# Suffix sums of the stick-breaking attention: from F32 products of the softplus to products of a rounded high part and a rest

## Chip, cores and metric

One core of a Trainium2 chip runs the whole program. The metric is the device time of one execution in microseconds (us); the median of three runs of the kernel before is 2748.29 us. Lower is better.

## What is computed

The reference is one inference step of a four-layer decoder trunk (S5, stick-breaking attention, chunked gMLP, S5, each followed by a SwiGLU block) for 512 prompt tokens and 8 sample tokens with 512 cached positions each. The change is in the attention of layer 1 alone:

```python
def sb_attend(q, k, v, q_pos, k_pos, bias):
    z = (jnp.einsum('bqhd,bkhd->bhqk', q, k).astype(jnp.float32) * (SB_HEAD_DIM ** -0.5)
         + bias.astype(jnp.float32)[None, :, None, None])
    mask = k_pos[None, :] < q_pos[:, None]
    log_not = jnp.where(mask, jax.nn.log_sigmoid(-z), 0.0)
    suffix = lax.cumsum(log_not, axis=3, reverse=True)
    log_w = jax.nn.log_sigmoid(z) + suffix - log_not
    w = jnp.where(mask, jnp.exp(log_w), 0.0).astype(v.dtype)
    return jnp.einsum('bhqk,bkhd->bqhd', w, v)
```

Since `log_sigmoid(z) - log_not` is `z`, a weight is `exp(z - S)`, where `S` is the sum of `softplus(z)` over the keys from this one on. The kernel makes `S` on TensorE: a product with a lower triangle of ones sums inside a block of 128 keys, and products with an all-ones matrix add the later blocks.

## The kernel before

Activations lie with 128 features on the partitions and the 520 tokens (512 prompt, 8 sample) as columns. Every projection is made from a high part rounded to FP32R and a rest: three matmuls for each weight tile of 128x128 and each half of the tokens (`mm`, lines 235, 236, 238). Weights come from HBM as `raw`, ScalarE rounds them to `wh` (L206) and VectorE subtracts to get `wl` (L208).

The attention stage (`attend`, L1385) runs three things at once, as generators that a planner resumes after so many microseconds of its own count of TensorE work (`self.t`, the numbers `SBH` and `SBY`); a scheduler then sets the final order on every engine.

- The query, key and value projections of the 8 head pairs (`full`).
- `sb_pipe` (L1273) for the prompt, head pair by head pair (`m` = 0 to 7), in three pieces `u` of key blocks, of 512, 384 and 384 query columns for each of the two heads. `scores(m, u)` makes the logits in PSUM, ScalarE adds the bias into `z` (L1318) and makes Abs, Exp and Ln in `e` (L1320 to L1322), VectorE completes the softplus (L1323). `weights(m, u)` multiplies `e` by the triangle `C["tri"]` (L1334) and by ones for the later key blocks (L1338), VectorE subtracts the sums from `z` (L1343), and ScalarE makes the exponential (L1344). `values(m)` multiplies `z` by the values (L1352).
- `sb_sample` (L1147) for the 8 sample tokens: 32 pages of cached keys and 32 of values are gathered by DMAs that POOL issues (L1154). POOL multiplies a page of keys by the query (L1190, two halves), VectorE reduces it (L1194); after each 8 pages come softplus and a small suffix sum (L1216, L1217), and then the products with the value pages (L1227).

For each head pair `z` of every piece has two buffers and `e` of every piece one; the key pages have four. In one head pair the suffix sums take, for each of two heads, 512 + 384 + 384 columns with the triangle and 768 + 384 + 128 with ones:

```python
later = {0: ((1, 0, 384, 128), (2, 0, 256, 256), (2, 256, 128, 384)),
         1: ((2, 0, 256, 128), (2, 256, 128, 256)), 2: ((2, 256, 128, 128),)}[u]
```

(piece, first column, columns, target column). Operands are F32, as the triangle and `self.ones` are.

## Time and profile before

| | us |
|---|---|
| median of three runs (lowest, highest) | 2748.29 (2747.35, 2749.26) |
| the profiled execution's own time | 2746.49 |
| its span in the profile | 2744.8 |
| TensorE busy over the span | 2576.6 (94%) |
| VectorE, ScalarE, POOL busy over the span | 1545.9, 1012.0, 459.1 |
| attention stage, first scores to last values | 755.8 to 1063.3 |

The span is what the profiler saw of the engines; 1.7 us of the execution lie around it. A matmul's end is modelled, so consecutive matmuls overlap in the list; how fast a run of them goes is read from start to start. An F32 matmul stands as two records, one in FP32R as one.

### The profile page before, as it was taken

The page shows a single profiled execution, that of the slowest core. Times are in us where ns is not written, and L with a number is a line of the kernel's source. Part 1 is how long each engine was busy: PE and PEld are TensorE (multiplying, and loading weights), DVE is VectorE, ACT ScalarE, POOL GpSimd, SP SyncE. Part 2 cuts the span into 40 slices and gives each one's busy share as a digit, 9 for nine tenths or more (in the row PEclk, how much of TensorE's full clock was granted, in tenths as well). Part 3 has the DMA queues.
Part 4 walks back from the last instruction along what each step waited for, and adds up shares of the span by engine and source line. Part 5 has one row for each costly group of instructions (what it writes and reads, how often), then busy time and mean ns, then how long its engine had stood idle before and what let it go on. Part 6 is the DMA issues. An engine that isn't in the chain of part 4 may idle for free.

```text
span 2744.8 us, 49994 instructions
## 1 busy us (share of the span) xinstructions
PE 2576.6 (94%) x20922; PEld 2457.4 (90%) x20922; DVE 1545.9 (56%) x2703; ACT 1012.0 (37%) x1713; POOL 459.1 (17%) x487
## 2 busy tenths in 40 slices
PE   7769999999998899999999989999999889999998
PEld 6659999999986667999999889999999779999998
DVE  8883553434647854734345778565646755634344
ACT  5443333222344454432223564433324333432222
POOL 5661210000128820300000203000001111200000
PEclk8879999999999999999999999999999999999999
DMA  4533223333147643233333333344333544233331
GB/s 118 146 87 90 80 80 106 93 93 91 41 134 243 222 147 93 66 103 94 93 92 63 90 101 90 114 135 141 116 110 123 167 129 124 66 104 92 90 90 46
DMA packets 483073, 295.48 MB, mean 108 GB/s; under 512 B 52296, under 2 KB 458080, under 8 KB 482848
## 3 DMA queue, kind: packets, MB, share of 16 engines
q1 hardware_dynamic: 473632, 258.73, 33.1%
q0 software_dynamic: 9216, 33.56, 3.5%
q8 instruction: 165, 2.70, 0.4%
q14 instruction: 60, 0.49, 0.1%
HBM read 262.51 MB, written 29.72 MB: 106 GB/s over the span
## 4 chain that ended last, share of the span: by engine, by line
PE 73%; DVE 11%; DMA 5%; ACT 4%; POOL 3%; issue 2%; SPq 0%; ACTq 0%; DVEq 0%; POOLq 0%
PE pp L235 22%; PE pp L236 22%; PE pp L238 22%; POOL kp L1190 1%; DVE wl L208 1%; DMA raw<-in_w_ffn_in_dram 1%; DVE pn L423 1%; DVE x L425 1%; ACT wh L206 1%; PE pp L1338 1%; PE pp L1334 1%; DVE hm L925 1%; POOL x L425 1%; DMA rot<-rotd 1%; DMA wn<-wnd 1%
## 5 line engine op out<-in xcount | busy, mean ns | idle before, releaser
L235 PE MATMUL pp<-xh,wh 128*128 128x264 f32 (+1 forms) x4480 | 1209.0, 288 | 26.5 <-DVE u L1008 6.0
L236 PE MATMUL pp<-xl,wh 128*128 128x264 f32 (+1 forms) x4480 | 1210.6, 286 | 6.6 <-DVE xl L408 6.4
L238 PE MATMUL pp<-xh,wl 128*128 128x264 f32 (+1 forms) x4480 | 992.7, 286 | 6.2 <-POOL wl L208 5.6
L235 PEld LDWEIGHTS pp<-xh,wh 128*128 128x128 f32 x4480 | 853.5, 191 | 40.9 <-issue 14.1
L236 PEld LDWEIGHTS pp<-xl,wh 128*128 128x128 f32 x4480 | 854.5, 191 | 11.9 <-DVE xl L408 9.7
L206 ACT ACTIVATE wh<-raw 128x1024 fp32r<-128x1024 f32 (+2 forms) x384 | 391.3, 1023 | 1080.4 <-PE pp L236 724.7
L238 PEld LDWEIGHTS pp<-xh,wl 128*128 128x128 f32 x4480 | 738.7, 191 | 9.7 <-POOL wl L208 5.8
L208 DVE TENSOR_TENSOR wl<-raw,wh 128x1024 fp32r<-128x1024 f32 (+2 forms) x364 | 442.6, 1218 | 292.8 <-ACT wh L206 290.2
L236 PE MATMUL pp<-hl,wh 128*128 128x256 f32 (+1 forms) x1408 | 377.2, 283 | 0.0
L235 PE MATMUL pp<-hh,wh 128*128 128x256 f32 (+1 forms) x1408 | 376.7, 284 | 0.0
L238 PE MATMUL pp<-hh,wl 128*128 128x256 f32 (+1 forms) x1408 | 312.9, 283 | 0.0
L235 PEld LDWEIGHTS pp<-hh,wh 128*128 128x128 f32 x1408 | 265.1, 188 | 1.2 <-issue 1.2
L236 PEld LDWEIGHTS pp<-hl,wh 128*128 128x128 f32 x1408 | 265.3, 188 | 0.0
L238 PEld LDWEIGHTS pp<-hh,wl 128*128 128x128 f32 x1408 | 230.7, 188 | 0.0
L1622 DVE TENSOR_TENSOR tg<-pp,rs 128x520 f32<-128x520 f32 (+2 forms) x100 | 62.5, 632 | 215.4 <-PE pp L238 215.3
L1633 DVE TENSOR_TENSOR tg<-pp,tg 128x520 f32<-128x520 f32 (+2 forms) x96 | 62.4, 652 | 209.2 <-PE pp L238 208.6
L1645 DVE TENSOR_TENSOR op<-pp,op 128x520 f32<-128x520 f32 (+2 forms) x96 | 54.0, 563 | 168.1 <-PE pp L238 167.9
L340 POOL TENSOR_TENSOR acc<-acc,s 128x256 f32<-128x256 f32 (+1 forms) x96 | 83.7, 872 | 99.2 <-ACT s L336 95.3
L208 POOL TENSOR_TENSOR wl<-raw,wh 128x1024 fp32r<-128x1024 f32 x20 | 48.2, 2414 | 303.6 <-ACT wh L206 274.4
L407 ACT ACTIVATE xh<-x,gt 128x264 fp32r<-128x264 f32 (+1 forms) x128 | 63.0, 505 | 60.8 <-DVE x L425 42.5
L408 DVE SCALAR_TENSOR_TENSOR xl<-x,gt,xh 128x264 fp32r<-128x264 f32 (+1 forms) x128 | 76.7, 615 | 1.4 <-ACT xh L407 1.2
L336 ACT ACTIVATE sq<-op 128x256 f32<-128x256 f32 (+2 forms) x72 | 32.6, 453 | 101.4 <-DVE op L1645 68.4
(342 smaller groups left out, 2701.0 us busy)
## 6 DMA issues: line engine op xcount, KB each, us to landing
raw<-in_w_ffn_in_dram SPq DMA_DIRECT2D x176, 512.0 KB
raw<-in_w_ffn_out_dram SPq DMA_DIRECT2D x48, 512.0 KB
raw<-in_w_ffn_out_dram SPq DMA_DIRECT2D x48, 384.0 KB
raw<-in_w_ssm_glu_dram SPq DMA_DIRECT2D x32, 512.0 KB
raw<-in_w_sb_qkv_dram SPq DMA_DIRECT2D x24, 512.0 KB
raw<-in_w_ssm_in_dram SPq DMA_DIRECT2D x16, 512.0 KB
raw<-in_w_cm_in_dram SPq DMA_DIRECT2D x16, 512.0 KB
cad<-caw SPq DMA_DIRECT2D x16, 288.0 KB
```

The source lines that it names most:

```text
L206: nc.scalar.activation(wh[:, :nk], raw[:, :nk], AF.Copy)
L208: on.tensor_tensor(wl[:, :nk], raw[:, :nk], wh[:, :nk], op=ALU.subtract)
L235: nc.tensor.matmul(ps(*h), lhsT=wh[:, k, :], rhs=xh[:, h[0]:h[1]], start=first, stop=False)
L236: nc.tensor.matmul(ps(*h), lhsT=wh[:, k, :], rhs=xl[:, h[0]:h[1]], start=False, stop=False)
L238: nc.tensor.matmul(ps(*h), lhsT=wl[:, k, :], rhs=xh[:, h[0]:h[1]], start=False, stop=last)
L340: i = (nc.gpsimd if pool else nc.vector).tensor_tensor(acc[0][:, c0:c1], acc[0][:, c0:c1], sq[:, :n], op=ALU.add)
L407: nc.scalar.activation(xs[k][0][:, c0:c1], self.x[k][:, c0:c1], AF.Copy, scale=g)
L408: return nc.vector.scalar_tensor_tensor(xs[k][1][:, c0:c1], self.x[k][:, c0:c1], g, xs[k][0][:, c0:c1], op0=ALU.mult, op1=ALU.subtract)
L425: add.tensor_tensor(self.x[k][:, c0:c1], self.x[k][:, c0:c1], t[:, :n], op=ALU.add)
L1622: v.tensor_tensor(g, ps(c0, c1), rs[:, c0:c1], op=ALU.mult)
L1633: v.tensor_tensor(t, ps(c0, c1), t, op=ALU.mult)
L1645: v.tensor_tensor(o, ps(c0, c1), o, op=ALU.add)
```

## The change

The softplus `e` is split as the activations of the projections are: ScalarE copies it into an FP32R tile `h` and VectorE writes the difference into an FP32R tile `l`. Each F32 product with the triangle or with ones becomes two FP32R products, one of `h` and one of `l`, which add up in PSUM. Triangle and ones are held in FP32R; the sample's small sums read the same matrices as F32. To make room, `e` is one tile for the three pieces, `z` of pieces 0 and 1 has one buffer and not two, the key pages have three buffers and not four, and some small tiles share buffers of the pool `nrm`. `values(m)` is issued ahead of `scores(m + 1, 1)`, where it stood behind it.

```diff
     def consts(self):
...
-        self.ones = c.tile([128, 128], F32, name="ones")
-        nc.vector.memset(self.ones, 1.0)
+        one = self.nrm.tile([128, N], F32, tag="sq", name="one")[:, :128]
+        nc.vector.memset(one, 1.0)
+        self.onesr = c.tile([128, 128], F32R, name="ones")
+        nc.vector.tensor_copy(self.onesr, one)
+        self.ones = self.onesr.bitcast(F32)
...
     def sb_consts(self, p):
...
-        C["tri"] = p.tile([128, 128], F32, name="atri")
-        nc.gpsimd.affine_select(out=C["tri"], in_=self.ones, pattern=[[-1, 128]], compare_op=ALU.is_ge, fill=0.0,
+        tri = self.nrm.tile([128, N], F32, tag="sq", name="atri")[:, :128]
+        nc.gpsimd.affine_select(out=tri, in_=self.ones, pattern=[[-1, 128]], compare_op=ALU.is_ge, fill=0.0,
                                 base=0, channel_multiplier=1)
+        C["tri"] = p.tile([128, 128], F32R, name="atrir")
+        nc.vector.tensor_copy(C["tri"], tri)
...
-        pg = p.tile([128, 32], I32, name="apg")
+        pg, io = (self.nrm.tile([128, 264], F32, tag="pn", name="apg")[:, :32].bitcast(I32) for _ in range(2))
         nc.sync.dma_start(pg, self.i["page_table"].rearrange("b c -> (b c)").partition_broadcast(128))
-        io = p.tile([128, 32], I32, name="aio")
...
     def sb_sample(self, qf, C, p, res, first):
...
-            t = p.tile([128, D], F32, tag=nm, name=nm, bufs=4 if nm == "kp" else 3)
+            t = p.tile([128, D], F32, tag=nm, name=nm, bufs=3)
...
         def scores(m, u):
...
-            z = T[m]["z", u] = p.tile([128, 2 * n], F32, tag=f"z{u}", name=f"z{u}")
-            e = T[m]["e", u] = p.tile([128, 2 * n], F32, tag=f"e{u}", name=f"e{u}", bufs=1)
+            z = T[m]["z", u] = p.tile([128, 2 * n], F32, tag=f"z{u}", name=f"z{u}", bufs=1 + (u > 1))
+            e = p.tile([128, 1024], F32, tag="e", name="e", bufs=1)[:, :2 * n]
...
             v.scalar_tensor_tensor(e, z, 0.0, e, op0=ALU.max, op1=ALU.add)
+            hi = T[m]["h", u] = p.tile([128, 2 * n], F32R, tag=f"h{u}", name=f"h{u}", bufs=1)
+            nc.scalar.activation(hi, e, AF.Copy)
+            lo = T[m]["l", u] = p.tile([128, 2 * n], F32R, tag=f"l{u}", name=f"l{u}", bufs=1)
+            v.tensor_tensor(lo, e, hi, op=ALU.subtract)
 
         def weights(m, u):
...
-                nc.tensor.matmul(o[:, :n], lhsT=C["tri"], rhs=T[m]["e", u][:, n * h:n * h + n], start=True, stop=False)
+                for q in "hl":
+                    nc.tensor.matmul(o[:, :n], lhsT=C["tri"], rhs=T[m][q, u][:, n * h:n * h + n], start=q == "h", stop=False)
...
-                    nc.tensor.matmul(o[:, to:to + x], lhsT=self.ones, rhs=T[m]["e", w][:, W[w] * h + c:W[w] * h + c + x],
-                                     start=False, stop=(w, c) == later[-1][:2])
+                    for q in "hl":
+                        nc.tensor.matmul(o[:, to:to + x], lhsT=self.onesr, rhs=T[m][q, w][:, W[w] * h + c:W[w] * h + c + x],
+                                         start=False, stop=q == "l" and (w, c) == later[-1][:2])
...
             if old:
                 weights(m, 0)
                 yield SBH[1]
+            if old:
+                values(m)
             if new:
                 scores(m + 1, 1)
                 yield SBH[2]
-            if old:
-                values(m)
-            if new:
                 weights(m + 1, 2)
```

The scheduler makes a new order of the attention stage from this; the rest of the program keeps its order. Three places matter. In the rows that follow a name before the arrow is what is written, `L` numbers of the changed kernel are 3 to 10 higher than those before.

On POOL, where the sample part begins (the gathers of key pages and their products), before:

```order
L1154 DMA kp<-in_cache_k_dram,arow 128x1024 x4
L1291 COPY smpk<-kf_7606 128x8
L1190 TENSOR_TENSOR kp<-kp,qb 128x512 x8
L1291 COPY smpv<-v 128x8
L1154 DMA kp<-in_cache_k_dram,arow 128x1024 x4
L1190 TENSOR_TENSOR kp<-kp,qh 128x512 x2
L1291 COPY smpk<-kf_7605 128x8
L1190 TENSOR_TENSOR kp<-kp,qh 128x512 x6
L1154 DMA kp<-in_cache_k_dram,arow 128x1024 x4
```

and now:

```order
L1158 DMA kp<-in_cache_k_dram,arow 128x1024 x3
L1295 COPY smpk<-kf_7608 128x8
L1194 TENSOR_TENSOR kp<-kp,qb 128x512 x6
L1295 COPY smpv<-v 128x8
L1158 DMA kp<-in_cache_k_dram,arow 128x1024 x3
L1194 TENSOR_TENSOR kp<-kp,qb 128x512 x2
L1194 TENSOR_TENSOR kp<-kp,qh 128x512 x2
L1295 COPY smpk<-kf_7607 128x8
L1194 TENSOR_TENSOR kp<-kp,qh 128x512 x2
L1158 DMA kp<-in_cache_k_dram,arow 128x1024 x3
```

Pages are gathered and multiplied in bursts of three instead of four.

On VectorE, around the first softplus of the sample part (`em`), between two weight splits (`wl`), before:

```order
L208 TENSOR_TENSOR wl<-raw,wh 128x1024
L1203 TENSOR_SCALAR em<-zs 128x128
L1206 TENSOR_TENSOR em<-em 128x128
L1208 MEMSET em 128x2x16
L1425 TENSOR_TENSOR v<-pp,rs 128x520
L1210 TENSOR_TENSOR em<-em 128x2x16 x3
L1194 TENSOR_REDUCE zs<-kp 128x16
L1343 TENSOR_TENSOR z_8673<-z_8673,pp 128x768
L1323 SCALAR_TENSOR_TENSOR e_8779<-z_8778,e_8779 128x1024
```

and now:

```order
L1207 TENSOR_SCALAR em<-zs 128x128
L1198 TENSOR_REDUCE zs<-kp 128x16
L1327 SCALAR_TENSOR_TENSOR e<-z_8824,e 128x1024
L1210 TENSOR_TENSOR em<-em 128x128
L1212 MEMSET em 128x2x16
L1214 TENSOR_TENSOR em<-em 128x2x16 x3
L1331 TENSOR_TENSOR l_8834<-e,h_8832 128x1024
L1426 TENSOR_TENSOR kf_7608<-pp,rs 128x520
L1223 TENSOR_TENSOR zs<-zs,pss 128x128
L211 TENSOR_TENSOR wl<-raw,wh 128x1024
L1198 TENSOR_REDUCE zs<-kp 128x16
```

The new subtract (L1331) stands a few instructions behind the softplus that it splits, with reductions of key pages (L1198) and a weight split (L211) in the same queue behind it.

On TensorE, the sums of piece 0 of head pair 6, before:

```order
L1334 MATMUL pp<-e_10268,atri 128x512 x2
L1338 MATMUL pp<-e_10172,ones 128x384
L1338 MATMUL pp<-e_10100,ones 128x256
L1338 MATMUL pp<-e_10100,ones 128x128
L1338 MATMUL pp<-e_10172,ones 128x384
L1338 MATMUL pp<-e_10100,ones 128x256
L1338 MATMUL pp<-e_10100,ones 128x128
```

and now:

```order
L1343 MATMUL pp<-h_10477,atrir 128x512
L1313 MATMUL pp<-q,kf_7608 128x384 x2
L1316 LDWEIGHTS amnb
L1316 MATMUL pp<-aidb,amnb 128x128
L1316 LDWEIGHTS amnb
L1316 MATMUL pp<-aidb,amnb 128x128
L1343 MATMUL pp<-l_10479,atrir 128x512
L1343 MATMUL pp<-h_10477,atrir 128x512
L1343 MATMUL pp<-l_10479,atrir 128x512
L1348 MATMUL pp<-h_10384,ones 128x384
L1348 MATMUL pp<-l_10386,ones 128x384
L1348 MATMUL pp<-h_10283,ones 128x256
```

There are twice as many products, and the first one of `h` stands ahead of other work (here the next scores) that fills the time until `l` is there.

## Rows read from the trace of the kernel before

**Rows 1.** The page: shares of the span in the chain that ended last.

```profile
PE 73%; DVE 11%; DMA 5%; ACT 4%; POOL 3%; issue 2%; SPq 0%; ACTq 0%; DVEq 0%; POOLq 0%
```

**Rows 2.** PE, PEld, DVE, ACT, POOL busy (count), 808 to 965 us; clock, DMA.

```profile
808.00:965.00 157.00, 138.51 (x912) 98.99 (x912) 121.13 (x119) 72.67 (x110) 136.51 (x119) 0.95 0.68 223
```

**Rows 3.** TensorE over time, piece 0 of pair 6: start, length, line, count.

```profile
1029.56 1.94 PE L1334 MATMUL pp<-e,atri 128*128 128x512 f32 x4
1031.34 2.76 PE L1338 MATMUL pp<-e,ones 128*128 128x384 f32 x12
1034.03 0.64 PE L1227 MATMUL psv<-vp,zs 128*32 128x256 f32 x8
```

**Rows 4.** TensorE over time, a projection behind the stage: 34 such starts.

```profile
1098.09 0.28 PE L236 MATMUL pp<-xl,wh 128*128 128x264 f32 x1
...
1102.09 0.28 PE L236 MATMUL pp<-xl,wh 128*128 128x264 f32 x1
```

**Rows 5.** Instructions on e by stretch: PE, PEld, DVE, ACT busy (count); clock.

```profile
808.00:965.00 157.00, 39.43 (x144) 25.91 (x144) 19.30 (x12) 32.94 (x36) 0.95 0.68 223
965.00:1066.00 101.00, 32.90 (x124) 21.05 (x124) 9.41 (x9) 24.65 (x27) 1.00 0.35 106
```

**Rows 6.** Groups of ScalarE in the stage: count | busy, mean ns of one.

```profile
L1320 ACT ACTIVATE e<-z 128x768 f32<-128x768 f32 x16 | 13.5, 843 | 34.4 <-PE pp L1338 34.2
...
L1320 ACT ACTIVATE e<-z 128x1024 f32<-128x1024 f32 x8 | 8.6, 1070 | 0.0
```

**Rows 7.** VectorE over time before POOL works: the softplus, two sizes.

```profile
765.42 0.96 DVE L1323 SCALAR_TENSOR_TENSOR e<-z,e 128x768 f32<-128x768 f32 x1 [1.53 <-ACT e L1322]
...
775.02 1.22 DVE L1323 SCALAR_TENSOR_TENSOR e<-z,e 128x1024 f32<-128x1024 f32 x1 [1.64 <-ACT e L1322]
```

**Rows 8.** Groups of VectorE while POOL multiplies pages, 808 to 965 us.

```profile
L208 DVE TENSOR_TENSOR wl<-raw,wh 128x1024 fp32r<-128x1024 f32 x9 | 21.1, 2346 | 1.5 <-ACT wh L206 1.5
...
L1206 DVE TENSOR_TENSOR em<-em 128x128 f32<-128x128 f32 x3 | 8.8, 2920 | 0.9 <-ACT em L1205 0.8
```

**Rows 9.** VectorE and POOL in order of time around one weight split.

```profile
901.94 6.45 DVE L208 TENSOR_TENSOR wl<-raw,wh 128x1024 fp32r<-128x1024 f32 x1
...
902.19 2.51 POOL L1190 TENSOR_TENSOR kp<-kp,qh 128x512 f32<-128x512 f32 x2
...
904.79 2.50 POOL L1190 TENSOR_TENSOR kp<-kp,qh 128x512 f32<-128x512 f32 x2
```

**Rows 10.** POOL over time: last gather of a burst, and the next product.

```profile
823.26 0.94 POOL L1154 DMA_INDIRECT kp<-in_cache_k_dram,arow  x1 [0.30 <-issue]
825.44 2.67 POOL L1190 TENSOR_TENSOR kp<-kp,qh 128x512 f32<-128x512 f32 x2 [1.23 <-DMA kp<-in_cache_k_dram,arow]
```

**Rows 11.** POOL in order of time: its last product of a key page.

```profile
962.47 2.54 POOL L1190 TENSOR_TENSOR kp<-kp,qh 128x512 f32<-128x512 f32 x2
```

**Rows 12.** TensorE over time: the last small suffix sum of the sample.

```profile
997.48 0.39 PE L1216 MATMUL pss<-em,atri 128*128 128x128 f32 x2
```

**Rows 13.** TensorE in order of time: values of head pair 4 and of 5.

```profile
978.59 2.37 PE L1352 MATMUL po<-z,tokv 128*64 128x512 f32 x16
...
1011.19 2.37 PE L1352 MATMUL po<-z,tokv 128*64 128x512 f32 x16
```

**Rows 14.** All engines in order of time: the end of head pair 7.

```profile
1049.77 1.23 DVE L1323 SCALAR_TENSOR_TENSOR e<-z,e 128x1024 f32<-128x1024 f32 x1 [0.92 <-ACT e L1322]
...
1051.05 1.98 PE L1334 MATMUL pp<-e,atri 128*128 128x512 f32 x4 [3.19 <-DVE e L1323]
...
1060.89 2.37 PE L1352 MATMUL po<-z,tokv 128*64 128x512 f32 x16
```

**Rows 15.** VectorE in order of time just ahead of the stage.

```profile
740.87 0.19 DVE L1132 SCALAR_TENSOR_TENSOR arow<-apg,aio 128x32 int32<-128x32 int32 x1
...
742.72 0.16 DVE L359 TENSOR_SCALAR v<-psn 128x2 f32<-128x2 f32 x1 [1.00 <-PE psn L357]
```

**Rows 16.** TensorE's first instruction of the program.

```profile
7.02 0.45 PE L113 MATMUL psg<-ident,g 128*128 128x128 f32 x1 [7.02 <-DMA pin<-in_ssm_lambda_im_dram]
```

More of the change, by code (lines that the diff above doesn't have):

```diff
@@ L1215, in weights @@
             ps = self.bk.tile([128, 512], F32, tag="b", name="pss")[:, :128]
-            nc.tensor.matmul(ps, lhsT=C["tri"], rhs=em[:, 128:256], start=True, stop=False)
+            nc.tensor.matmul(ps, lhsT=C["tri"].bitcast(F32), rhs=em[:, 128:256], start=True, stop=False)
             nc.tensor.matmul(ps, lhsT=self.ones, rhs=em[:, :128], start=False, stop=True)
@@ L1237, in times_v @@
                 v.tensor_tensor(av, av, C["own"].unsqueeze(2).to_broadcast([128, 4, 64]), op=ALU.mult)
-                sums[b] = p.tile([128, 64], F32, tag="sv", name="sv")
+                sums[b] = p.tile([128, 64], F32, tag="sv", name="sv", bufs=1)
                 v.tensor_reduce(sums[b], av.rearrange("p i d -> p d i"), axis=AX.X, op=ALU.add)
@@ L1454, in attend @@
             self.t += 0.5
-            so = p1.tile([128, D], F32, tag="kp", name="so", bufs=4)
+            so = p1.tile([128, D], F32, tag="kp", name="so", bufs=3)
             nc.scalar.activation(so[:NS], pt[:NS], AF.Copy)
```

## Prediction

> **What bounds the kernel now.** I read the chain of waits first: TensorE holds 73% of what ended last [rows 1], so a saving on TensorE counts wherever nothing else ends later. The change touches the attention stage alone, so I then read the busy time by stretch and the order of time there. The stage has three stretches. From 755 to 808 us TensorE works through query projections. From 808 to 965 us POOL multiplies the key pages of the samples: POOL is busy 136.5 of 157 us, VectorE 121.1, TensorE 138.5, and the clock granted to TensorE is 0.95, where 1.00 is the higher of its two levels, 2.4 GHz [rows 2]. No engine alone sets this stretch: the reader is to see three queues that hand work to each other. From 965 to 1066 us POOL is done [rows 11], the clock is 1.00 [rows 5], and head pairs follow each other at 32.6 us (the values of pairs 4 and 5, [rows 13]) and then at 24.9 us (from pair 5 at 1011.19 to pair 7 at 1060.89 us, two steps, [rows 13, 14]). There TensorE sets the pace.
>
> **The products.** For piece 0 the columns per head are 512 + 768, for both heads 2560; its products run from 1029.56 to 1034.03 us, 4.47 us, which is 1.75 ns a column [rows 3]. One head pair has 2 x (1280 + 1280) = 5120 columns, eight have 40,960: 71.5 us of F32 products. An FP32R product of 264 columns starts every 0.121 us (33 steps from 1098.09 to 1102.09 us), 0.46 ns a column [rows 4]. Two of them for one F32 product cost 0.92 ns a column, 37.6 us: 34 us less.
>
> The unknown is the short product. Three pieces in each head have 128 columns: 48 F32 products, 96 FP32R ones. No FP32R product in the trace is below 256 columns. By columns one costs 0.059 us. At worst it costs what the F32 product of as many columns does, 0.22 us, 15.5 us more in all. I take 0.121 us, the nearest row of its kind [rows 4], since each product loads its weights anew, loads and products being as many [rows 2]: 96 x 0.062 = 6 us more. TensorE thus has **28 us** less to do (18.5 to 34). The Trainium skill, "TensorE: Matmul & The Clock Gate", section on LDWEIGHTS, says that a weight load takes as long as its columns at 1.2 GHz, whatever the rows: an estimate of 0.107 us for 128 columns, which would bind a product of 128 columns; the sum by it would be 29 us less. No row here shows it for so short a product.
>
> The 144 F32 products on `e` are 288 records, of which 144 lie in the middle stretch and 124 behind it [rows 5], so 20 ahead of it: 14.0, 12.1 and 1.9 us of the 28.
>
> **The split.** It adds 24 copies on ScalarE, 16 of 0.84 us and 8 of 1.07 us (the Abs of the same size, [rows 6]), 22 us, and 24 subtracts on VectorE, 16 of 0.96 us and 8 of 1.22 us (the softplus of the same size, [rows 7]), 25 us. Both lie between the softplus and its products, so each piece is ready some 2 us later plus what its queues hold. The new order lets `h` of the triangle go first and puts other work ahead of `l`.
>
> From 755 to 808 us the queues of both engines are short; I keep the whole 1.9 us.
>
> From 965 us on, other products cover the split, but for the last pair, whose piece 0 is a chain with nothing beside it: softplus at 1049.77, sums at 1051.05, values at 1060.89 us [rows 14]. Its sums get 2.3 us shorter (half of 4.5) and the split adds 1.07 + 1.22. So 12.1 - 2.3 = 9.8 us remain. The single buffers of `z` close a loop: from the sums of piece 0 over subtract, exponential, values, then bias, Abs to Ln, softplus, copy and subtract of piece 1, the same of piece 0, to the next sums. By the rows of these sizes (1.22, 1.06, 2.4; 1.1, 2.5, 0.96, 0.84, 0.96; 3.2, 1.22, 1.07, 1.22; 2.3) that is 20 us. Pairs now take 25 to 33 us and would take 21 to 29: the loop just fits, with nothing over for a queue. The bounds for this stretch are therefore 0 and 12.1.
>
> From 808 to 965 us lie 12 of the 24 subtracts (as many as softplus there, [rows 5]). Undisturbed they are 4 x 1.22 + 8 x 0.96 = 12.6 us. But VectorE instructions with two SBUF inputs stretch here: the weight split takes 2.35 us on the mean, a 128-column addition 2.92 us [rows 8], and one split that begins at 901.94 us takes 6.45 us, until POOL's products that begin at 902.19 have passed [rows 9]. At the split's mean of 2.35 for 1.22 us the 12 subtracts cost 24 us. VectorE has 36 us of idle time in the stretch [rows 2]. The price on the path is between 0 (idle time takes it) and 45 us (each also waits as the 128-column addition does: 128 of the 768 columns that take 0.96 us would be 0.16, so 2.7 us of its 2.92 are waiting). With 11 us of copies on ScalarE in the same chains, I take 14 us, a little over half of the 24: nothing of the 14.0 us saved there is left.
>
> **The rest.** Key pages come in bursts of three: behind a burst of four POOL waits 1.23 us for the first page [rows 10], behind three about 2.5, since one gather less (0.94 us and 0.30 ahead of it) covers it. Some four such bursts give 5 us and as many as 10 all through, on POOL. The cover: the last small sum of the sample runs at 997.48 us [rows 12], 32 us behind POOL's last product at 965.0 [rows 11]. If TensorE came to that sum 20 us sooner, it would still fit, so I take 0 (0 to 5). The page table now waits for a buffer of `nrm` and behind two weight loads on SP's queue; its user on VectorE runs at 740.87 us, and what stands behind it waits for TensorE until 742.72 us anyway [rows 15]: 0, at most 1.5 us. The extra copy of the ones, at the start, hides behind the DMA that TensorE waits for until 7.02 us [rows 16]. Moving `values` ahead of `scores` lets `z` be freed early; it adds no work.
>
> **Sum.** -1.9 - 9.8 + (14 - 14.0) = -11.7 us from the profiled execution's own 2746.5: 2734.8. The median shown is 1.8 us above that execution, so the forecast is **2737 us**.
>
> **Rivals.**
> - *All of it comes through* (-28 us, 2720). For it: VectorE's idle time in the middle stretch, and the scheduler's products of `h` that wait for nothing. Against it: [rows 8], and the loop of 20 us. It needs the split to cost nothing in any queue.
> - *Nothing is left* (2743 to 2753). The loop holds the pairs at their old pace from 965 us on, or the short products cost 0.22 us each and take another 9.5 us. For it: the pairs' 24.9 us against 20 with no queue; no row for the short products.
> - *Slower by VectorE's queue.* Place: 808 to 965 us. A subtract has two SBUF inputs; when POOL multiplies, it holds VectorE's queue until POOL pauses, and with it the reduction behind it, for which POOL's next gather waits now that only three key pages have buffers. At the upper price, 45 us for 12 subtracts, the stretch gets 31 us longer and the whole 31 - 11.7 = 19 us: 2767 us. It decides against the kernel once a subtract costs the path 2.6 us or more: (14.0 + 11.7 + 5.5) / 12. For it: 2.92 and 6.45 us in [rows 8, 9]. Against it: the softplus itself stands in the same queue, and its 12 instructions took 19.3 us there, 1.6 each [rows 5]. The Trainium skill, "SBUF — State Buffer", section "Who interferes with whom", has this as a rule: a VectorE instruction with two SBUF inputs and a GpSimd instruction that reads SBUF exclude each other, and the second waits for the whole of the first. The trace agrees in [rows 9], 6.45 us where the same split takes some 1.2 us. By the rule POOL also waits when a subtract comes first, up to 1.2 us for each of the 12, which would move POOL's last product, not the sum above.
> - *The rounded products don't run in one pass.* Then TensorE gains nothing and the split is all cost. The projections' products of the same type start every 0.121 us [rows 4], so I give it 1 in 100.
>
> **How the numbers follow.** About 0.2% (5.5 us) is what a measurement of this kernel can tell from no change. The forecast's case, 6 to 22 us faster, gets 0.48 (its own range: 2726 to 2743), all of it or nearly 0.10, no change 0.22, slower 0.20 with the failed pass in it. So faster 0.58, same 0.22, slower 0.20. The range 2721 to 2756 leaves out the best 6 in 100 and the worst 13.
>
> **What would show it.** Of the products: lines with `h` and `l` at 0.92 ns a column for both together, and 128-column ones starting every 0.12 us. Of the last stretch: values of the last three pairs 21 to 29 us apart. Of the middle stretch: the stage's POOL part still ends 155 to 165 us after it began, the new subtract at a mean near 2 us there, and VectorE busy above 140 us. I am wrong if the pairs keep their old pace behind 965 us, if the middle stretch gets shorter by as much as TensorE saves, or if the subtract's mean goes beyond 2.6 us and the key pages end 20 us later or more.

## The result: 14 us slower, and the profile after

The changed kernel took 2761.71 us (median of 5 runs, 2760.23 to 2767.26), the kernel before 2749.26 us in 5 runs beside it. The ratio is 1.0051, 95% interval 1.0036 to 1.0065: slower by 14 us (10 to 18). The forecast was 2737 us with a range of 2721 to 2756, so it was wrong, on the slow side. The profiled execution took 2760.23 us of its own time, 2758.5 us of span.

TensorE's share of the chain that ended last fell from 73% [rows 1]. The page of the changed kernel:

```profile
PE 70%; DVE 11%; DMA 6%; ACT 4%; issue 3%; POOL 3%; SPq 0%; another core or an unknown queue 0%; ACTq 0%; DVEq 0%; POOLq 0%
```

The stage begins when it did, and its last values come 15.1 us later than at 1060.89 us [rows 14]; the span grew by 13.7 us, so the loss is the stage's. TensorE in order of time, the values of pairs 4, 5 and 7 (lines move by 3 to 10: values are now L1362, the products L1343 and L1348, copy L1329, subtract L1331, reduction L1198, page gather L1158):

```profile
982.85 2.38 PE L1362 MATMUL po<-z,tokv 128*64 128x512 f32 x16
...
1018.93 1.40 PE L1362 MATMUL po<-z,tokv 128*64 128x512 f32 x6
...
1076.02 1.40 PE L1362 MATMUL po<-z,tokv 128*64 128x512 f32 x6
```

The values of pair 4 lose 4.3 us against 978.59 [rows 13]; the three pairs behind them take 93.2 us in place of 82.3. So 4 us are lost up to the end of the sample part and 11 behind it, where 9.8 were to be gained. The dividing line at pair 4 is not quite like for like: counted by line in both traces, 46 more of the projections' products now stand ahead of it (from pair 0 on) and 26 fewer behind it, at 0.12 us each [rows 4] 5.6 and 3.1 us. The loss behind pair 4 is rather larger than 11 us.

**The products did what was forecast.** TensorE in order of time, piece 0 of pair 5, products with the ones:

```profile
1011.45 0.34 PE L1348 MATMUL pp<-h,ones 128*128 128x384 f32 x1
...
1012.03 0.22 PE L1348 MATMUL pp<-h,ones 128*128 128x128 f32 x1
1012.09 0.27 PE L1348 MATMUL pp<-l,ones 128*128 128x128 f32 x1
1012.20 0.39 PE L1348 MATMUL pp<-h,ones 128*128 128x384 f32 x1
...
1012.90 0.27 PE L1348 MATMUL pp<-l,ones 128*128 128x128 f32 x1
1013.01 0.33 PE L238 MATMUL pp<-xh,wh 128*128 128x256 f32 x1
```

Twelve products take 1.56 us (1011.45 to 1013.01) for what took 2.69 us in F32 [rows 3]. Two short ones take 0.17 us (1012.03 to 1012.20), 0.085 each; I had taken 0.121. The Trainium skill, "TensorE: Matmul & The Clock Gate", section "Back-to-back issue gap", gives about 81 ns a product for 128 columns in a stream of loads and products; this row agrees.

**Where the saving went.** Busy time by stretch, from the values of pair 0 to those of pair 4, and from there to those of pair 7. Columns: stretch, length, busy time with count of PE, PEld, DVE, ACT, POOL, then TensorE's granted clock (1.00 is 2.4 GHz), DMA share, GB/s. The kernel before:

```profile
825.00:978.59 153.59, 135.10 (x890) 94.33 (x889) 118.57 (x121) 72.92 (x111) 125.55 (x111) 0.94 0.67 222
978.59:1060.89 82.30, 78.03 (x537) 52.49 (x536) 37.64 (x66) 49.45 (x82) 11.51 (x14) 1.00 0.36 110
```

The changed kernel:

```profile
822.60:982.85 160.25, 133.02 (x935) 101.51 (x934) 133.58 (x131) 83.71 (x122) 133.93 (x113) 0.88 0.67 219
982.85:1076.02 93.17, 75.47 (x512) 52.53 (x511) 47.16 (x77) 58.20 (x92) 14.57 (x16) 0.84 0.30 97
```

Busy time times granted clock is an estimate of the work done. Before it is 135.10 x 0.94 + 78.03 = 205.0 us, after 133.02 x 0.88 + 75.47 x 0.84 = 180.5: **24.5 us less work**. But busy time itself fell only from 213.1 to 208.5, so by this estimate the lower clock took back 19.9 us. Idle time grew from 22.8 to 44.9 us, by 22.1. The sum, -24.5 + 19.9 + 22.1 = 17.5 us, is what these two stretches grew by. Behind the sample part the clock fell where TensorE stood idle, or just after; before, it stayed at 1.00 there throughout, also in the stretch with the most idle time:

```profile
1040.00:1050.00 10.00, 7.17 (x38) 4.51 (x37) 5.73 (x16) 8.94 (x21) 0.00 (x0) 1.00 0.20 54
```

The changed kernel, ten us each:

```profile
990.00:1000.00 10.00, 7.60 (x39) 4.29 (x39) 4.77 (x12) 5.27 (x10) 2.87 (x3) 0.56 0.73 217
...
1040.00:1050.00 10.00, 9.13 (x58) 6.25 (x57) 4.30 (x5) 4.45 (x7) 0.00 (x0) 0.88 0.00 0
1050.00:1060.00 10.00, 4.32 (x25) 3.14 (x24) 4.58 (x14) 8.83 (x21) 0.00 (x0) 0.80 0.19 52
1060.00:1070.00 10.00, 6.73 (x29) 4.73 (x28) 3.32 (x3) 4.75 (x5) 0.00 (x0) 0.51 0.05 8
```

TensorE is busy 4.32 of 10 us from 1050 us on, and in the next 10 us its mean clock is 0.51, nearly all of it at the lower level.

**What TensorE waited for behind the sample part.** The waits of TensorE from 965 to 1080 us, the longest (total, times, longest):

```profile
PE pp L1343 <- ACT h L1329: 9.4, 4, 3.3
```

So it is `h` that is late, not `l` (0.3 us in all); before, the same place waited 3.2 us, for the softplus. All engines in order of time, from one Abs of a piece 0 (pair 6) to the next (pair 7):

```profile
1029.59 1.06 ACT L1324 ACTIVATE e<-z 128x1024 f32<-128x1024 f32 x1 [0.98 <-DVE accv L1238]
...
1034.91 1.06 ACT L1329 ACTIVATE h<-e 128x1024 fp32r<-128x1024 f32 x1 [0.49 <-DVE e L1327]
...
1036.02 0.80 PE L1343 MATMUL pp<-h,atrir 128*128 128x512 f32 x1 [2.97 <-ACT h L1329]
...
1036.75 1.65 PE L1313 MATMUL pp<-q,kf 64*128 64x384 f32 x4
...
1042.82 1.22 DVE L1353 TENSOR_TENSOR z<-z,pp 128x1024 f32<-128x1024 f32 x1 [1.98 <-PE pp L1348]
...
1044.08 1.06 ACT L1354 ACTIVATE z<-z 128x1024 f32<-128x1024 f32 x1 [0.52 <-DVE z L1353]
...
1046.35 2.37 PE L1362 MATMUL po<-z,tokv 128*64 128x512 f32 x16
...
1048.20 2.19 ACT L1322 ACTIVATE z<-pp,abias 128x512 f32<-128x512 f32 x4
...
1050.74 0.87 ACT L1324 ACTIVATE e<-z 128x768 f32<-128x768 f32 x1
...
1056.60 0.96 DVE L1331 TENSOR_TENSOR l<-e,h 128x768 fp32r<-128x768 f32 x1 [0.30 <-ACT h L1329]
...
1057.59 1.06 ACT L1324 ACTIVATE e<-z 128x1024 f32<-128x1024 f32 x1 [1.02 <-DVE l L1331]
```

This loop takes 28.0 us, a pair's whole period (the pairs here are 27.4 and 29.7 us apart). Its last step shows the shared `e`: the `z` of piece 0 was there at 1050.39 us (1048.20 + 2.19), but its Abs starts at 1057.59, when the subtract of piece 1 has let `e` go.

**The middle stretch.** POOL's last product of a key page starts at 980.36 us, not at 962.47 [rows 11], 18 us later. The last small sum is two products, one with the triangle, which [rows 12] shows, and one with the ones. The second of them before, then both in the changed kernel:

```profile
1000.15 0.38 PE L1217 MATMUL pss<-em,ones 128*128 128x128 f32 x2
```

```profile
995.48 0.76 PE L1220 MATMUL pss<-em,atrir 128*128 128x128 f32 x2 [1.76 <-DVE em L1210]
...
1005.15 0.39 PE L1221 MATMUL pss<-em,ones 128*128 128x128 f32 x2
```

The first comes 2 us sooner than before, the second 5 us later; of the 32 us between POOL's end and the first, 12 are left. VectorE's groups from 808 to 965 us, the softplus before and then the changed kernel:

```profile
L1323 DVE SCALAR_TENSOR_TENSOR e<-z,e 128x1024 f32<-128x1024 f32 x4 | 10.7, 2686 | 0.0
L1323 DVE SCALAR_TENSOR_TENSOR e<-z,e 128x768 f32<-128x768 f32 x8 | 8.6, 1070 | 0.5 <-ACT e L1322 0.5
```

```profile
L211 DVE TENSOR_TENSOR wl<-raw,wh 128x1024 fp32r<-128x1024 f32 x9 | 27.8, 3094 | 1.0 <-ACT wh L209 0.8
L1327 DVE SCALAR_TENSOR_TENSOR e<-z,e 128x768 f32<-128x768 f32 x8 | 16.7, 2088 | 0.0
L1331 DVE TENSOR_TENSOR l<-e,h 128x768 fp32r<-128x768 f32 x8 | 9.0, 1125 | 0.9 <-ACT h L1329 0.9
L1327 DVE SCALAR_TENSOR_TENSOR e<-z,e 128x1024 f32<-128x1024 f32 x4 | 4.9, 1224 | 1.2 <-ACT e L1326 1.2
```

The new subtract takes 1.1 us, not the 2 I had expected. The weight split goes from 2.35 [rows 8] to 3.09 us and the softplus of 768 columns from 1.07 to 2.09, but that of 1024 columns falls from 2.69 to 1.22 us. What is stretched has changed places.

### The profile page after: what moved, and what is told of

Its sections match the earlier page's. It is cut to its first block, busy times and chain, and to the rows that moved or that the text cites. A ratio compares the mean times of both kernels' runs of the same rounds, so it can differ in the third digit from the quotient of the medians.

```text
span 2758.5 us, 50052 instructions
## 1 busy us (share of the span) xinstructions
PE 2565.2 (93%) x20922; PEld 2458.8 (89%) x20922; DVE 1572.4 (57%) x2729; ACT 1033.9 (37%) x1737; POOL 467.7 (17%) x487
## 4 chain that ended last, share of the span: by engine, by line
PE 70%; DVE 11%; DMA 6%; ACT 4%; issue 3%; POOL 3%; SPq 0%; another core or an unknown queue 0%; ACTq 0%; DVEq 0%; POOLq 0%
PE pp L238 22%; PE pp L239 21%; PE pp L241 21%; DMA raw<-in_w_ffn_in_dram 2%; DVE wl L211 1%; POOL kp L1194 1%; ACT wh L209 1%; DVE pn L426 1%; DVE x L428 1%; DMA wn<-wnd 1%; PE pp L937 1%; POOL x L428 1%; DVE hm L928 1%; PE pp L936 1%; PE pp L1343 1%
## 5 line engine op out<-in xcount | busy, mean ns | idle before, releaser
L211 DVE TENSOR_TENSOR wl<-raw,wh 128x1024 fp32r<-128x1024 f32 (+2 forms) x364 | 451.3, 1242 | 298.3 <-ACT wh L209 295.4
L211 POOL TENSOR_TENSOR wl<-raw,wh 128x1024 fp32r<-128x1024 f32 x20 | 48.2, 2418 | 316.2 <-ACT wh L209 275.2
```

The lines of the kernel that those rows point to most:

```text
L211: on.tensor_tensor(wl[:, :nk], raw[:, :nk], wh[:, :nk], op=ALU.subtract)
```

## The experiments

Ratios are against the kernel before, run beside each; 0.1% is 2.75 us. Two accounts stood against each other: **the split** costs the time (by VectorE's work, by ScalarE's copy, or by the loop over `e`), or **the room** made for it does (three key buffers, single `z`, order of values). Each edit also makes the scheduler find another order for the stage: of POOL's 154 instructions there, 152 stand in e14 in the order that they have in e1, but 117 in e13 and 116 in e5, counted from the traces. So a price below is that of an edit together with its order; no run held the order fixed.

### e1: no split

```diff
-            v.scalar_tensor_tensor(e, z, 0.0, e, op0=ALU.max, op1=ALU.add)
-            hi = T[m]["h", u] = p.tile([128, 2 * n], F32R, ...)
-            nc.scalar.activation(hi, e, AF.Copy)
-            lo = T[m]["l", u] = p.tile([128, 2 * n], F32R, ...)
-            v.tensor_tensor(lo, e, hi, op=ALU.subtract)
+            hi = T[m]["h", u] = T[m]["l", u] = p.tile([128, 2 * n], F32R, ...)
+            v.scalar_tensor_tensor(hi, z, 0.0, e, op0=ALU.max, op1=ALU.add)
```

> The changed kernel without the split: VectorE writes the softplus rounded straight into h, and every product reads h, twice, so copy and subtract are gone while the number and form of the products, all buffers and the order stay. (The rest is left out and the high part counted twice.) Accounts of the 40 us between the 28 us that the products should save and the 12 us that were lost: if the split itself costs them (ScalarE held 34 us in front of its copies, TensorE 24 us in front of h), this runs at 2722 to 2740 us; if the room made for it costs them (three key buffers, one z for the first two blocks, one e, values earlier), it stays at 2752 to 2762.

Measured: 2731.37 us, ratio 0.9925 (0.9901 to 0.9948), 21 us under before and, by the ratios, 35 under the change. Taking the split out gives this back, so the split is the cost. The same two stretches:

```profile
820.20:957.70 137.50, 121.98 (x896) 93.84 (x895) 105.13 (x116) 72.25 (x108) 118.66 (x104) 0.95 0.72 241
957.70:1040.30 82.60, 72.72 (x522) 53.39 (x521) 44.22 (x71) 52.55 (x85) 23.91 (x24) 0.90 0.41 129
```

The work is 181.3 us by the same estimate, near the change's 180.5, with 25.4 us of idle time, near the 22.8 of before. (These stretches hold 31 fewer products of the projections than the change's, some 3.7 us, so the estimate is good to some 5 us.) Even so the last three pairs take 82.6 us: with 12 us less to do TensorE idles more there, and its clock falls from 1.00 to 0.90.

### e2: the room alone

```diff
-            z = T[m]["z", u] = p.tile([128, 2 * n], F32, tag=f"z{u}", name=f"z{u}")
+            z = T[m]["z", u] = p.tile([128, 2 * n], F32, tag=f"z{u}", name=f"z{u}", bufs=1 + (u > 1))
...
-            t = p.tile([128, D], F32, tag=nm, name=nm, bufs=4 if nm == "kp" else 3)
+            t = p.tile([128, D], F32, tag=nm, name=nm, bufs=3)
```

(and `values` ahead of the scores of block 1, as in the change; `e` keeps its three tiles)

> The kernel before with the room of the change alone: three key-page buffers, one z buffer for blocks 0 and 1, values ahead of the scores of block 1; products in F32 on e as before, no split, and e not shared (it must live until the products). If the split costs the time: within 4 us of before, 2745 to 2753. If the room costs it: 2765 to 2790.

Measured: 2754.03 us, ratio 1.0009 (0.9998 to 1.0020): some 2.5 us more, not told apart from none, and 1 us above what was expected if the split costs. The room is nearly free as long as nothing else is added.

### e3: the copy on VectorE

```diff
-            nc.scalar.activation(hi, e, AF.Copy)
+            v.tensor_copy(hi, e)
```

> The changed kernel with the rounding copy on VectorE, so that softplus, copy and subtract follow each other on one engine and ScalarE is never held behind VectorE. If ScalarE's queue (34 us held in front of the copies) is what slows the pairs: 2738 to 2752. If VectorE's own work is the bound (24 more operations of about 0.8 us in an engine busy 126 of 157 us): 2765 to 2785.

Measured: 2769.02 us, ratio 1.0065 (1.0047 to 1.0082), against 1.0051 of the change. It is no faster. This does not part two cases: ScalarE's being held behind the softplus may cost nothing, or the 24 more operations on VectorE may take back what it costs.

### e4: values in their old place

```diff
-            if old:
-                values(m)
             if new:
                 scores(m + 1, 1)
                 yield SBH[2]
+            if old:
+                values(m)
```

> The changed kernel with values back behind the scores of block 1, as before the change. If the single z buffers make ScalarE wait for values (11.8 us in the trace of the change), this makes it worse: 2768 to 2785. If the early place of values holds TensorE in front of work that was ready: 2750 to 2758.

Measured: 2775.88 us, ratio 1.0090 (1.0074 to 1.0107), 11 us more than the change. With one `z`, block 1's bias must wait for the values, and the move is needed. The change's own trace shows such a wait, behind the values of pair 5:

```profile
1020.70 1.05 ACT L1322 ACTIVATE z<-pp,abias 128x384 f32<-128x384 f32 x2 [2.86 <-PE po L1362]
```

### e5: the subtract aside

The edit is shown against e1.

```diff
             v.scalar_tensor_tensor(hi, z, 0.0, e, op0=ALU.max, op1=ALU.add)
+            lo = p.tile([128, 2 * n], F32, tag=f"l{u}", name=f"l{u}", bufs=1)
+            v.tensor_tensor(lo, z, hi, op=ALU.subtract)
```

> The kernel of e1 (VectorE writes the softplus rounded into h, products read h twice) with the subtract put back on VectorE off the chain: it takes z minus h into l, which nothing reads, so VectorE works as long as in the change and no product waits for it. e1 stood 20 us under before and 31 us under the change. If VectorE's work is the cost of the split, 20 us or more of the 31 come back: 2750 to 2762. If it is the steps that stand in the chain from softplus to product: 2729 to 2738.

Measured: 2753.54 us, ratio 1.0009 (0.9998 to 1.0021): 23 us above e1, though nothing reads the result: VectorE's added work costs that, with the order that it brings. From 808 to 965 us the subtract is stretched here, as it was not in the change:

```profile
L1330 DVE TENSOR_TENSOR l<-z,h 128x768 f32<-128x768 f32 x8 | 19.4, 2421 | 0.0
```

The two stretches:

```profile
822.40:983.57 161.17, 135.57 (x926) 105.76 (x925) 130.90 (x133) 72.40 (x109) 136.74 (x113) 0.86 0.66 216
983.57:1060.94 77.37, 67.54 (x502) 49.51 (x501) 44.55 (x75) 52.40 (x85) 11.32 (x14) 0.91 0.36 117
```

The first is as long as in the change (160.25), the second 15.8 us shorter. So the subtracts alone can account for the change's middle stretch, but not for its last three pairs.

### e6: the copy in the chain

The edit is shown against e1.

```diff
-            v.scalar_tensor_tensor(hi, z, 0.0, e, op0=ALU.max, op1=ALU.add)
+            v.scalar_tensor_tensor(e, z, 0.0, e, op0=ALU.max, op1=ALU.add)
+            nc.scalar.activation(hi, e, AF.Copy)
```

> The kernel of e1 with the softplus written in F32 to e and copied to h by ScalarE, as in the change, and no subtract: the products read h twice (the rest is left out, the high part counted twice). The chain has its hop to ScalarE and e is held until the copy, VectorE has nothing more to do than in e1. If the hop and the order of ScalarE's queue are the cost: 2745 to 2762. If VectorE's work is: 2729 to 2738.

Measured: 2737.49 us, ratio 0.9955 (0.9940 to 0.9970): 8 us above e1, with intervals that overlap, and in the range of the account by VectorE. Copy and hop are the smaller part.

### e7, e8 and e9: a second `e`, a fourth key page, neither

All three hold the rest `l` in BF16, with the triangle and ones in BF16 for its products. e7 spends the room on `e`, e8 on the key pages, e9 on nothing.

```diff
-            lo = T[m]["l", u] = p.tile([128, 2 * n], F32R, ...)
+            lo = T[m]["l", u] = p.tile([128, 2 * n], BF16, ...)
...
-            e = p.tile([128, 1024], F32, tag="e", name="e", bufs=1)[:, :2 * n]
+            e = p.tile([128, 1024], F32, tag="e", name="e", bufs=2)[:, :2 * n]
```

> The change with two buffers of the shared e, for which the rest l is written in BF16 (half the room; its products with the triangle and ones in BF16). If the single e, which closes a loop of six steps on two engines for every block (ScalarE waited 13 us for l), paces the last pairs: 2740 to 2752. If VectorE's work is the cost: 2757 to 2766.

> The change with the fourth key-page buffer back, for which the rest l is written in BF16. POOL's last key product came 18 us later in the change; if the three buffers did that and it sets the end: 2743 to 2752. If POOL is late because VectorE's reductions are: 2757 to 2764, with POOL's last key product again after 975 us.

> The change with the rest l in BF16 and its room left empty: a control for e7 and e8. If the second e alone made e7 faster: as the change, 2757 to 2765. If the BF16 rest itself is cheaper (its products, its stores): 2745 to 2752.

Measured: e7 2745.75 us, 0.9984 (0.9969 to 0.9999); e8 2759.58 us, 1.0036 (1.0025 to 1.0046); e9 2757.49 us, 1.0033 (1.0017 to 1.0049). The second `e` is worth 13 us over e9. The last three pairs in e9, then in e7:

```profile
975.61:1063.32 87.71, 70.84 (x513) 45.29 (x512) 47.25 (x78) 58.78 (x93) 14.22 (x16) 0.88 0.34 105
```

```profile
973.89:1053.97 80.08, 66.72 (x518) 44.19 (x520) 49.71 (x80) 57.84 (x93) 17.50 (x19) 0.94 0.40 126
```

The fourth key page gives nothing to the whole, although POOL begins the second half of its last key product at 965.8 us instead of 975.5 in e9; so e8 fits neither of its two accounts, with the time of the one and the POOL of the other. The values of pair 4 come no sooner either (978.50 us, 975.61 in e9), and the last three pairs need 88.9 us. That the loop over `e` hides the gain there is possible, but e10 speaks against it. The waits of ScalarE, longest first (total, times, longest), have this line in the change, and none on `l` in e7:

```profile
ACT e L1324 <- DVE l L1331: 13.3, 9, 4.1
```

That the BF16 rest is itself cheaper (5 us under the change) stays open: the intervals overlap.

### e10: both

```diff
-            hi = T[m]["h", u] = p.tile([128, 2 * n], F32R, ...)
+            hi = T[m]["h", u] = p.tile([128, 2 * n], BF16, ...)
```

(with the edits of e7 and the fourth key-page buffer)

> Both parts of the split in BF16, and the room that this leaves given to a second e and the fourth key-page buffer. In e8 the fourth buffer let POOL end the key products 15 us earlier and gave 4 us up to values(5), all lost again behind the single e. If each cost is a loop of its own, they add: 2734 to 2743. If VectorE's work bounds the middle whatever the buffers: as e7, 2743 to 2749.

Measured: 2743.92 us, ratio 0.9979 (0.9965 to 0.9993), not told apart from e7. A miss for the sum of the two: with the second `e` in place the fourth key page still gives nothing that can be told, so three key pages are not shown to cost the change anything.

### e11: the high part from z

This is e7 with `hi` in BF16 and `lo` in FP32R; the lines shown are against the change.

```diff
+            nc.scalar.activation(hi, z, AF.Relu)
             nc.scalar.activation(e, z, AF.Abs)
...
-            nc.scalar.activation(hi, e, AF.Copy)
```

> As e7 with two e, but the high part is max(z,0) rounded to BF16 by ScalarE straight from z, ahead of the Abs, and the rest (softplus minus that) goes rounded into l: as many operations on each engine, none of them on ScalarE behind VectorE. e6 priced the copy in the chain at 6 us. If that price is the order in the chain: 2736 to 2743. If it is ScalarE's time: 2743 to 2750.

Measured: 2750.87 us, ratio 1.0004 (0.9986 to 1.0022), not below e7 and just above both ranges expected, a miss. Taking the copy out from behind the softplus gains nothing here; its place is now ahead of the Abs in ScalarE's queue. That speaks for ScalarE's time rather than the hop as the price of e6, without showing it.

### e12: three products, no sum on VectorE

```diff
+            nc.scalar.activation(hi, z, AF.Relu)
+            nc.scalar.activation(ln, z, AF.Abs)
+            nc.scalar.activation(ln, ln, AF.Exp, scale=-1.0)
+            nc.scalar.activation(ln, ln, AF.Ln, bias=1.0)
+            v.scalar_tensor_tensor(lo, z, 0.0, hi, op0=ALU.max, op1=ALU.subtract)
```

(in place of the lines from Abs to the subtract; `hi` and `lo` in BF16, `ln` rounded to FP32R without a rest; no shared `e`)

> The softplus never added up on VectorE: ScalarE rounds max(z,0) to BF16 as high part, VectorE takes the rest of max(z,0) from it (one operation, in place of the softplus), and ln(1+exp(-abs z)) goes rounded from ScalarE into l; three products (20,480 columns and 96 short ones more, 14 us of TensorE by the estimate), VectorE as much work as before the change. If VectorE's added work is what the split costs: e1 plus what of the 14 us is on the path, 2731 to 2746. If TensorE's columns bound the stage: 2746 to 2760.

Measured: 2740.81 us, ratio 0.9969 (0.9956 to 0.9981): faster than both kernels, with three products where the change has two. The two stretches:

```profile
819.50:967.20 147.70, 128.81 (x957) 90.58 (x956) 109.04 (x117) 80.58 (x120) 129.51 (x111) 0.95 0.70 232
967.20:1050.90 83.70, 79.69 (x618) 53.47 (x617) 41.83 (x71) 57.88 (x94) 16.40 (x18) 0.98 0.37 115
```

A third product is 40,960 columns and 48 short ones more, not the 20,480 and 96 of the expectation: some 20 us at 0.46 ns a column and 0.085 us a short one, 17.5 of them in these stretches. The work is 200.5 us, 20 more than in the change, and it is done 22 us sooner (147.7 + 83.7 against 160.3 + 93.2): TensorE idles 22.9 us instead of 44.9, and its clock is 0.95 and 0.98 instead of 0.88 and 0.84.

### e13 and e14: the subtract aside, by stretch

The edit is shown against e1.

```diff
+            if m < 5:
+                lo = p.tile([128, 2 * n], F32, tag=f"l{u}", name=f"l{u}", bufs=1)
+                v.tensor_tensor(lo, z, hi, op=ALU.subtract)
```

(e14: `if m >= 5`)

> e5 (the subtract on VectorE, read by nothing) with the 15 subtracts of pairs 0 to 4 alone, which fall before POOL's last key products. All 24 cost 22 us. If VectorE's work costs where it stands beside POOL's key products and the reductions: 2746 to 2756. If it costs in the last pairs: 2730 to 2738.

> e5 with the nine subtracts of pairs 5 to 7 alone. If VectorE's work costs only beside the sample part: as e1, 2728 to 2736. If each subtract costs its own time wherever it stands: 2738 to 2744.

Measured: e13 2745.79 us, 0.9986 (0.9970 to 1.0002), 17 us above e1; e14 2731.32 us, 0.9926 (0.9904 to 0.9948), no different from e1. VectorE's work costs only beside the sample part here: 15 subtracts, 17 us, 1.1 each. In e13 the values of pair 4 come at 982.99 us, as late as in the change (982.85), against 957.67 in e1; the last three pairs then take 74.4 us.

### e15: the subtract aside, four key pages

The edit is shown against e5, whose `l` now has one tile for all pieces.

```diff
-            lo = p.tile([128, 2 * n], F32, tag=f"l{u}", name=f"l{u}", bufs=1)
+            lo = p.tile([128, 1024], F32, tag="l", name="l", bufs=1)[:, :2 * n]
...
-            t = p.tile([128, D], F32, tag=nm, name=nm, bufs=3)
+            t = p.tile([128, D], F32, tag=nm, name=nm, bufs=4 if nm == "kp" else 3)
```

> e5 with the fourth key-page buffer (the unread differences share one tile for it). If VectorE's work costs by way of POOL, which waits with its gathers for late reductions: back toward e1, 2730 to 2742. If it costs by VectorE's own order, softplus and z behind reductions and subtracts: 2746 to 2754.

Measured: 2740.30 us, ratio 0.9962 (0.9948 to 0.9976): 13 of e5's 23 us come back, as the account by POOL has it. POOL's waits from 808 to 965 us for the reduction on VectorE that frees a page (total, times, longest), in e5:

```profile
POOL kp L1158 <- DVE zs L1198: 8.1, 8, 2.7
```

and in e15:

```profile
POOL kp L1158 <- DVE zs L1198: 1.4, 5, 0.3
```

In e1 and in the change:

```profile
POOL kp L1158 <- DVE zs L1198: 0.9, 3, 0.3
```

```profile
POOL kp L1158 <- DVE zs L1198: 5.8, 4, 2.7
```

POOL's last product starts at 979.36 us in e5 and at 964.13 in e15. The subtract is no longer stretched either:

```profile
L1330 DVE TENSOR_TENSOR l<-z,h 128x768 f32<-128x768 f32 x9 | 10.8, 1204 | 0.0
```

So the 13 us may be POOL's waits or the stretching, and this run does not part them. What a fourth page gives to e1 itself was not run; its waits leave 0.9 us for it.

### e16: e12 with a second z of block 1

The edit is shown against e12.

```diff
-            z = T[m]["z", u] = p.tile([128, 2 * n], F32, tag=f"z{u}", name=f"z{u}", bufs=1 + (u > 1))
+            z = T[m]["z", u] = p.tile([128, 2 * n], F32, tag=f"z{u}", name=f"z{u}", bufs=1 + (u > 0))
```

> e12 with a second z buffer for block 1 in the room that is left there. e2 priced the single z of blocks 0 and 1 (with the key pages) at about 2 us: 2736 to 2742 if that is all; 2728 to 2735 if scores of block 1 wait for values in the faster pairs of e12.

Measured: 2737.09 us, ratio 0.9945 (0.9928 to 0.9963): 15 us faster than the kernel before, the best found of the kernels that keep the rest. The gain over e12 is within the intervals.

## Why the prediction was wrong

**The step that failed** is the one on the stretch behind 965 us, "the loop just fits, with nothing over for a queue", priced at 9.8 us of gain. The trace of the change shows that loop, step by step, closed at the end by the shared `e` where the forecast had named `z` alone. Its size was wrong: 20 us by the sum, 28.0 in the trace. The sums of piece 0, 2.3 us in the forecast, take 6.8 (from `h` at 1035.97 to 1042.8 us), because TensorE runs the next pair's scores in between and at a clock of 0.78 to 0.88. TensorE then comes to the values 1.2 us after their exponential is done. Bias and the way to the next Abs take 2.5 us instead of 1.1 (1048.20 to 1050.74), piece 1 from Abs to the end of its subtract 6.8 instead of 5.3, piece 0 from Abs to `h` 6.4 instead of 5.5. Only the subtract of piece 0, 1.2 us, and 0.5 us at the values were counted too much. I had added bare durations, on engines that serve the samples and the projections between them. A loop that fits by bare durations with 1 us to spare does not fit: 10.9 us were lost where 9.8 were to be gained, 20.7 of the 25.4 us by which the profiled execution missed the forecast. That the long chain is what costs here, e5 shows: VectorE has a subtract as often there, but no product waits for a copy or a rest, and these pairs take 77.4 us, 15.8 less than in the change. The single `e` is a part of that, 7.6 us in these pairs and 13 in the whole (e7 beside e9). The forecast needed 72.5 us, and no run came to that; how the other steps share the rest is read from the rows and was not tried.

**The middle stretch** was near the forecast in mechanism. Nothing of the 14.0 us saved there was to be left; the values of pair 4 came 4.3 us late instead of 1.9 early, with 5.6 us more of the projections ahead of them. My 14 us for 12 subtracts stands beside 17 us for 15 (e13), and the copy's 8 us (e6) come on top, most of which I had meant the 14 to hold. That the sum came near is in part luck: I had priced the subtract by its stretching, and in the change it was not stretched (1.1 us), though it was in e5 (2.4) and e13 (2.2). By which way the subtracts cost time in the change stays open. In e5 four key pages gave back 13 of 23 us; in the change they gave nothing (e8 and e9, e7 and e10). The 0 for the bursts of three held as far as it was measured (e2, 2.5 us with the rest of the room). The "last small suffix sum" at 997.48 us was not the last: the product with the ones followed at 1000.15.

**The products** were right, and 31 us by the measured spacing rather than 28 (96 short ones at 0.085 us). But less work was not as much less time: e1, without any split, gained 21 of the 31 us; the room may hold some 2.5 of the rest (e2). The step "12.1 us less behind 965 us" took the clock of 1.00 for granted; there it fell to 0.90 in e1 and 0.84 in the change. Before, TensorE idled 4.3 of 82.3 us there; with 12 us less to do it idled 9.9 in e1, and the clock went down with it.

**The rivals.** "Slower by VectorE's queue" named 2767 us, and the result is 2762; but its point of decision, 2.6 us a subtract on the path, was not reached (1.1 in e13). It put the whole loss between 808 and 965 us, but up to the values of pair 4 only 4 of the 15 us arose; its three key pages counted in e5 at most and not in the change; and it had no word of `e`. That its number came close is luck. "All of it comes through" is e1 and e14, which need the split gone. "Not one pass" is out by the rows of the products.

**What I had said would show it:** both products near 0.92 ns a column (1.02 in the rows above, short ones among them): right. The last pairs 21 to 29 us apart: 36.1, 27.4, 29.7, wrong; the first sign named for being wrong was that they keep their old pace (32.6 us, then twice 24.9), and they are slower still. POOL's part 155 to 165 us: from 808.8 to 983.1 us it is 174, wrong, and this is near the sign that I had named for a loss. VectorE busy above 140 us in the middle: 126.0, wrong.

Open: some 6 us between e5 and e13 plus e14, within their intervals; what the scheduler's orders add to each price; and how far the lower clock is a cost of its own or only follows the waits, since no run held the clock and changed the waits.

## What to carry to other kernels

When a saving on the pacing engine is paid for with steps elsewhere, write down the loop that each single buffer closes, with the queue waits that the trace shows for the same engines, not with bare durations. Here the loop was 28 us where bare durations made 20, so a loop that fills the period by such a sum is to be taken for longer than the period. A side engine that feeds another one's buffers (here VectorE, freeing POOL's pages) can be on the path beside it and free elsewhere: the same subtract cost 1.1 us in one stretch (e13) and nothing that could be told in the next (e14). Extra work for the pacing engine that keeps its chain short (e12) can beat less work behind a longer one.

## What the runs showed of the hardware

From the values of pair 4 to those of pair 7 TensorE's granted clock was 1.00 before, with 4.3 us idle. In the change, with 17.7 us idle there, it was 0.84: 0.56 from 990 to 1000 us, with 7.60 of 10 us busy, and 0.51 from 1060 us, after 10 us with 4.32 busy. In e12, with 4.0 us idle, it was 0.98. Idle time by itself does not settle it, since 7.17 of 10 us busy from 1040 us left the kernel before at 1.00. By the estimate above the lower clock gave back 19.9 of the 24.5 us of work saved over the two stretches.

The stretching of VectorE beside POOL fell on one instruction in one kernel and on another in the next. From 808 to 965 us the softplus of 1024 columns took 2.69 us on the mean before and 1.22 in the change, that of 768 columns 1.07 and 2.09, the weight split 2.35 and 3.09; the subtract of 768 columns took 1.1 us in the change, 2.4 in e5 and 1.2 in e15. The Trainium skill, "SBUF — State Buffer", section "Who interferes with whom", counts all three alike, as instructions with two SBUF inputs that exclude a GpSimd instruction reading SBUF. The rows agree for all three; which of them is hit no sum made here foretold. The split in [rows 9] ended 1.1 us behind the last of four products of POOL (904.79 + 2.50), so one instruction of VectorE can wait for several of POOL.
